# Eighteen query buffers in tiles of two groups, every store of two groups, and one gate for the accumulators

## The chip, the cores and the metric

The kernel runs on one core of a Trainium2 chip. A core has five engines with a queue of instructions each: TensorE (PE: matrix products into the accumulator memory PSUM), VectorE (DVE), ScalarE (ACT), GpSimd (POOL) and SyncE (SP, which here only issues transfers), and 16 DMA engines that move data between HBM and the on-chip memory SBUF. The engines run beside each other and are kept in step by semaphores alone. The metric is the device time of one execution in microseconds (us), lower is better. Three runs of the kernel before gave 128.72, 128.75 and 128.87 us, a median of 128.75.

## The reference

Every query of 8 x 12 heads attends to the same 16 keys and values of its head: those at positions 0, 64, 128, ... of 1024.

```python
def reference(Q, K, V, stride):                  # Q, K, V: (8, 12, 1024, 64) float32, stride 64
    attend_positions = np.arange(0, seq, stride)
    for i in range(seq):
        q = Q[:, :, i:i + 1, :]
        k = K[:, :, attend_positions, :]
        v = V[:, :, attend_positions, :]
        scores = np.einsum('bhqd,bhkd->bhqk', q, k) / np.sqrt(dim)
        weights = np.exp(scores - np.max(scores, axis=-1, keepdims=True))
        weights = weights / (np.sum(weights, axis=-1, keepdims=True) + 1e-10)
        result[:, :, i, :] = np.einsum('bhqk,bhkd->bhqd', weights, v)[:, :, 0, :]
```

Q is 25.2 MB and is read once, the result is as large and is written once. Of K and V only every 64th row is needed, 0.4 MB each.

## The kernel before, in words

**Tiling.** The 96 heads are taken as 24 groups of four heads (`NG` = 24). One group of Q is 1 MB, 2048 numbers on each of the 128 partitions. It is loaded into one of `BUFS` = 16 buffers `qn`, and when the group is done its output lies in the same buffer, from where it is stored. So group 16 can be loaded only when group 0 has been stored, since it takes the same buffer. The 16 buffers are four tiles `quad` of `RUN` = 4 buffers each, so that neighbouring groups lie side by side on a partition and one transfer (`send`) can store two or four of them.

**Stages of a group.** POOL casts the buffer to bf16 (`cast`, L306; the first three are shared with ACT, L300 and L302). DVE transposes it (L317). PE makes the scores in 16 products (`score_products`, L325). DVE takes the maximum and subtracts it (L339, L342). ACT takes the exponential (`raise_`, L347). DVE sums and inverts (L352, L355). POOL forms the weights (L359). PE transposes them in four products (`turn_products`, L366). ACT spreads them into a block form (`spread`, L378, two halves). PE multiplies with the values in eight products, four into either half of the accumulator tile `o` (`output_products`, L386). ACT copies the two halves of `o` to the buffer (`evict`, L406).

**The order.** The work is recorded in a fixed order, `ORDER`, one round per group, with a stage's number saying how many groups it lags. ACT's round is: spread of group i-3, eviction of both halves of group i-4, exponential of group i-1. PE runs a loop of two rounds per turn instead of a recorded list: scores of i, turning of i-2, output of i-3. The other engines' finished work reaches that loop through semaphores called gates: `turned` (DVE's transpose is there), `weighted` (POOL's weights are there), and `free0` and `free1` (ACT has emptied the first or the second half of `o`). The loop has 28 rounds for 24 groups; in the rounds past either end it multiplies data that nobody uses, and the tiles `k_t` and `v_all` are padded for them.

**Transfers.** All are issued by SP, in recorded order, through `_copy`, which builds the transfer instruction itself. First come the keys, group 0 of Q, the values, and groups 1 to 15. Then come the stores. `STORES` sets their sizes in groups, 4, 2, 2, 4, 4, 4, 2, 2; each is queued when its last group has been evicted. Behind the third store SP queues the loads of groups 16 to 23, each of which waits until the store of its buffer has landed. SP's queue is in order, so that nothing behind a waiting load is issued before it. The last store is sent from behind the recorded program, after all engines are done with it.

Of the kernel before, what the change touches and what calls it, by code (L numbers as in the profile page):

```python
# [10 lines left out]
FP32 = mybir.dt.float32  # L11
BF16 = mybir.dt.bfloat16
# [6 lines left out]
def _ap_with(ap: bass.AP, new_ap, extra_offset: int = 0) -> bass.AP:  # L19
    return dataclasses.replace(  # L20
        ap, ap=[list(p) for p in new_ap], offset=ap.offset + extra_offset
    )


def _copy(nc, out: bass.AP, in_: bass.AP):

    sides = [
        mybir.BassSymbolicTensorAccessPattern(
            ap=side.ap, dtype=side.dtype, bass_ap=side,
            is_dma=True, for_custom_bir_dma=True,  # L30
        )
        for side in (in_, out)
    ]
    return nc.sync.add_instruction(  # L34
        mybir.InstDMACopy(
            name=nc.get_next_instruction_name(), engine=mybir.EngineType.SP,
            ins=sides[:1], outs=sides[1:], queue="qSPDynamicHW",
            mode="Copy",
        )
    )  # L40


class Program:
# [125 lines left out]
def kernel(  # L169
# [29 lines left out]
    quads = [sb.tile([P, RUN, 32 * D], FP32, name=f"quad{i}") for i in range(BUFS // RUN)]  # L199
    qn = [quads[i // RUN][:, i % RUN] for i in range(BUFS)]  # L200
# [110 lines left out]
    def transpose(g):  # L311
        k_in = {0: "0", 1: "1"}.get(g)
        words = qt[g % 2].bitcast(I32)
        if g >= NG:
            op("DVE", lambda: nc.vector.memset(edge[:, g - NG : g - NG + 1], 0.0), gate="turned", times=1 if g == NG else 3)
# [42 lines left out]
    def weights(g):  # L358
        op("POOL", lambda: nc.gpsimd.tensor_tensor(  # L359
            out=wt[g % 2], in0=ex[g % 2],  # L360
            in1=rec[g % 2].unsqueeze(2).to_broadcast([P, 32, NK]), op=ALU.mult,
        ), reads=[f"ex{g % 2}", f"rec{g % 2}"] + [k for k in apart if k[0] == "v"], writes=[f"wt{g % 2}"], gate="weighted", times=1 if g < NG - 1 else 3)

    def turn_products(g):
        for c in range(4):
# [30 lines left out]
    def outputs(g, n):  # L396
        op("PE", None, reads=[f"wb{g % 2}0", f"wb{g % 2}1"] + [
               f"v{g % 2}{a}{b}{int(g >= 4)}" if 0 <= g < NG else "none" for a in range(2) for b in range(2)
           ], writes=[f"o{n}"], gates=[(f"free{n}", g + 1)] if g >= 0 else [], looped=True)

    def evict(g, n):
        to = qn[g % BUFS].rearrange("p (b c x d) -> p c b (x d)", b=2, c=4, d=D)
        half = slice(2 * n, 2 * n + 2)
        plain = g >= NG - 1 - 2 * n
        ready = [f"wb{(g + 1) % 2}0", f"wb{(g + 1) % 2}1"] * (n == 0)
        op("ACT", lambda: nc.scalar.copy(  # L406
            to[:, half], o_ps[:, half].rearrange("p c (b x) -> p c b x", b=2)
        ), reads=[f"o{n}"] + ready, writes=[f"qn{g % BUFS}{n}"],
           gate=None if plain else f"free{n}", last=g == NG - 1 and n == 1)

        if plain:
            free([f"qn{g % BUFS}{n}"], n)

    def free(reads, n):
        op("ACT", lambda: nc.scalar.nop(), reads=reads, gate=f"free{n}")  # L415

    def send(g, n):
        return _copy(
            nc,
            _ap_with(out, [[16 * D, P], [2 * SD, 2 * n], [1, 16 * D]], g * HG * SD),  # L420
            _ap_with(qn[g % BUFS], [quads[0].ap[0], [1, 1], [1, 32 * n * D]]),
        )

    def store(g, n):
# [40 lines left out]
    assert sum(STORES) == NG  # L465
    STORED = {sum(STORES[: i + 1]) - 1: n for i, n in enumerate(STORES)}

    def queue(g):
        if g not in STORED or g == NG - 1:
            return  # L470
        store(g - STORED[g] + 1, STORED[g])
        if g == NG - BUFS - 1:
            for n in range(BUFS, NG):
                load(n)

    def at(i, stage, lag):
        g = i - lag
        if g in early.get(stage, ()):
            return
        if stage == "transpose" and 0 <= g < NG + 2:  # L480
            transpose(g)
        elif stage == "scores" and 0 <= g < NG + 4:
            scores(g)
        elif stage == "weights" and 0 <= g < NG:
            weights(g)
        elif stage == "turn" and 0 <= g < NG + 2:
            turn(g)
        elif stage in ("outA", "outB") and -1 <= g < NG + 1:
            outputs(g, int(stage == "outB"))
        elif stage == "spread" and 0 <= g < NG:  # L490
            spread(g)
        elif stage in ("evA", "evB") and g == -1:
            n = int(stage == "evB")
            free(["wb00", "wb01"], n)
# [17 lines left out]
    def pe_stream(sems, gates):  # L512
        pe = nc.tensor
        done = sems["PE"]
        pe.sem_inc(gates["weighted"], 2)
        for n in range(2):
            pe.sem_inc(gates[f"free{n}"], 3)
        with pe.Fori(0, turns) as turn_:
            for j in range(TURN):
                i = turn_ * TURN + j  # L520
                pe.wait_ge(gates["turned"], j + 1)
                score_products(j, i).then_inc(done, 1)
                pe.wait_ge(gates["weighted"], j + 1)
                turn_products(j).then_inc(done, 1)
                for n in range(2):
                    pe.wait_ge(gates[f"free{n}"], j + 1)
                    output_products(j + 1, i, n).then_inc(done, 1)
            for name in ("turned", "weighted", "free0", "free1"):
# [11 lines left out]
_INS = ['Q', 'K', 'V', 'stride']  # L540
# [31 lines left out]
```

## Time and profile before

| | before |
|---|---|
| median of three runs | 128.75 us |
| the profiled execution: its time | 128.75 us |
| its span (first instruction to last) | 126.9 us |
| mean granted clock of TensorE | 0.86 |
| read, written | 25.95 MB, 25.17 MB |
| busy: PE / DVE / ACT / POOL | 66.9 / 88.0 / 97.6 / 75.9 us |

The span leaves out 1.85 us of the execution's time, which lie around it. The profile's page shows busy time by engine, the span in 40 slices of 3.17 us (a digit is the busy share in tenths), the DMA queues with the time that their packets took as a share of 16 engines' span, and the chain of work that ended last. A window table gives the same by stretches; its last two columns are the share of the 16 DMA engines that was busy (it can pass 1 for a short while, where one packet begins before the last one has ended) and the rate. In a timeline a row has its start, its length, engine, line, operation, tiles, and in brackets how long the engine had been idle and what released it. "SPq" is SyncE's queue: its rows are the issuing of transfers, not the transfers themselves.

### The profile page before, as it was taken

How to read it: one execution, taken by the hardware profiler on the slowest of the kernel's cores; microseconds unless marked ns; L12 is line 12 of the kernel's file. 1: busy time of each engine (PE TensorE's matmuls, PEld its weight loads, DVE VectorE, ACT ScalarE, POOL GpSimd, SP SyncE). 2: the span in 40 equal slices, each digit the busy share in tenths (PEclk: the TensorE clock that was granted, in tenths of full speed). 3: DMA queues.
4: the chain of work that ended last, by engine and by line, in shares of the span. 5: the costliest groups of instructions: out<-in, count | busy, mean ns of one | idle time of the engine just before them, and what ended most of it. 6: DMA issues, size and time to landing. Idle time of an engine off the chain costs nothing.

```text
span 126.9 us, 2253 instructions
## 1 busy us (share of the span) xinstructions
PE 66.9 (53%) x784; PEld 49.3 (39%) x784; DVE 88.0 (69%) x131; ACT 97.6 (77%) x133; POOL 75.9 (60%) x67
## 2 busy tenths in 40 slices
PE   0005796677836456586530394557856478771000
PEld 0004585455734334364320373335624356550000
DVE  3585979999899999999980779999999773000000
ACT  4147758999999999999993199999999999991000
POOL 5637698999999777797403996777793332000000
PEclk9999999965799999959996579998599955999755
DMA  0999999899998989989999999999999999999980
GB/s 23 418 320 465 392 454 465 372 475 392 444 475 361 465 361 485 454 351 423 418 470 434 413 454 392 465 434 403 454 385 457 423 423 444 392 398 434 429 382 21
DMA packets 5413, 51.16 MB, mean 403 GB/s; under 512 B 3616, under 2 KB 3616, under 8 KB 3616
## 3 DMA queue, kind: packets, MB, share of 16 engines
q1 hardware_dynamic: 5408, 51.12, 95.8%
q14 instruction: 5, 0.04, 0.1%
HBM read 25.95 MB, written 25.17 MB: 403 GB/s over the span
## 4 chain that ended last, share of the span: by engine, by line
DMA 30%; ACT 22%; POOL 21%; DVE 6%; issue 6%; PE 4%; SPq 1%; ACTq 0%; POOLq 0%
DMA out_dram<-quad 14%; ACT quad L406 13%; POOL qb L306 12%; DMA quad<-in_Q_dram 10%; ACT wb_all L378 7%; POOL wt_all L359 6%; DMA v_raw<-in_V_dram 6%; DVE qt L317 3%; ACT ex L347 3%; POOL v_all L288 2%; PE o L386 2%; DVE total L352 1%; SPq L34 1%; PE tp L366 1%; DVE top L339 1%
## 5 line engine op out<-in xcount | busy, mean ns | idle before, releaser
L406 ACT COPY quad<-o 128x1024 f32<-128x1024 f32 x48 | 46.3, 1015 | 2.2
L306 POOL CAST qb<-quad 128x2048 bf16<-128x2048 f32 x21 | 39.7, 1889 | 6.9 <-DMA quad<-in_Q_dram 6.8
L386 PE MATMUL o<-v_all,wb_all 128*128 x224 | 39.0, 317 | 2.4 <-ACTq L415 0.7
L359 POOL TENSOR_TENSOR wt_all<-ex,rec 128x512 bf16<-128x512 f32 x24 | 25.4, 1057 | 18.5 <-DVE rec L355 18.1
L378 ACT ACTIVATE wb_all<-tp,sel 128x512 bf16<-128x512 bf16 x48 | 30.4, 690 | 5.6 <-PE tp L366 5.4
L317 DVE STREAM_TRANSPOSE qt<-qb 128x1024 int32<-128x1024 int32 x24 | 29.7, 1237 | 5.2 <-POOL qb L306 5.0
L325 PE MATMUL sc<-k_t,qt 128*128 x448 | 23.3, 210 | 16.2 <-DVE qt L317 11.8
L325 PEld LDWEIGHTS sc<-k_t,qt 128*128 128x128 bf16 x448 | 20.4, 109 | 21.8 <-issue 19.6
L366 PE MATMUL tp<-identity,wt_all 128*128 128x128 bf16 x112 | 13.0, 249 | 29.8 <-POOL wt_all L359 29.8
L386 PEld LDWEIGHTS o<-v_all,wb_all 128*128 128x128 bf16 x224 | 22.9, 114 | 11.2 <-ACT quad L406 4.9
L352 DVE TENSOR_REDUCE total<-ex 128x32 f32<-128x512 f32 x24 | 16.3, 677 | 7.0 <-ACT ex L347 7.0
L366 PEld LDWEIGHTS tp<-identity,wt_all 128*128 128x128 bf16 x112 | 7.6, 109 | 32.6 <-POOL wt_all L359 32.6
L342 DVE TENSOR_TENSOR low<-sc,top 128x512 f32<-128x512 f32 x24 | 16.6, 691 | 0.8
L347 ACT ACTIVATE ex<-low 128x512 f32<-128x512 f32 x24 | 15.4, 641 | 2.1 <-DVE low L342 2.0
L339 DVE TENSOR_REDUCE top<-sc 128x32 f32<-128x512 f32 x24 | 15.2, 632 | 1.3 <-PE sc L325 1.3
L355 DVE RECIPROCAL rec<-total 128x32 f32<-128x32 f32 x24 | 8.5, 353 | 0.8
L288 POOL CAST v_all<-v_raw 32x128 bf16<-32x128 f32 (+1 forms) x12 | 5.2, 430 | 1.1 <-DMA v_raw<-in_V_dram 0.4
L302 POOL CAST qb<-quad 128x1024 bf16<-128x1024 f32 x3 | 3.1, 1037 | 4.3 <-DMA quad<-in_Q_dram 4.2
L300 ACT CAST qb<-quad 128x1024 bf16<-128x1024 f32 x3 | 3.1, 1045 | 2.4 <-DMA quad<-in_Q_dram 2.4
L264 ACT CAST k_half<-k_raw 128x768 bf16<-128x768 f32 x1 | 0.8, 831 | 3.2 <-DMA k_raw<-in_K_dram 3.2
L260 POOL MEMSET v_all<- 128x3584 f32 x1 | 3.1, 3085 | 0.0
L288 ACT CAST v_all<-v_raw 32x640 bf16<-32x640 f32 x4 | 2.9, 722 | 0.0
(15 smaller groups left out, 10.3 us busy)
## 6 DMA issues: line engine op xcount, KB each, us to landing
quad<-in_Q_dram SPq DMA_DIRECT2D x24, 1024.0 KB, 17.3
out_dram<-quad SPq DMA_DIRECT2D x4, 4096.0 KB, 18.3
out_dram<-quad SPq DMA_DIRECT2D x4, 2048.0 KB, 12.8
k_raw<-in_K_dram SPq DMA_DIRECT2D x1, 384.0 KB, 4.9
v_raw<-in_V_dram SPq DMA_DIRECT2D x1, 384.0 KB, 7.0
```

The lines of the kernel that those rows point to most:

```text
L306: op("POOL", lambda: nc.gpsimd.tensor_copy(out=b, in_=q), reads=[f"qn{g % BUFS}{h}" for h in range(2)] + apart, writes=[f"qb{g % 2}{h}" fo ...
L317: op("DVE", lambda: nc.vector.transpose(_ap_with(words, [words.ap[0], [1, 2], [D, 16], [2, 32]]), qb[g % 2].bitcast(I32),), reads=[f"qb{g ...
L325: r = nc.tensor.matmul(sc_ps[g % 2][:, 64 * i : 64 * i + 64], lhsT=_ap_with(qt[g % 2], [qt[g % 2].ap[0], [2, P]], extra_offset=2 * P * i + f),
L339: op("DVE", lambda: nc.vector.tensor_reduce(out=m, in_=s, op=ALU.max, axis=mybir.AxisListType.X,), reads=[f"sc{g % 2}"], writes=[f"top{g % ...
L342: op("DVE", lambda: nc.vector.tensor_tensor(out=low, in0=s, in1=m.unsqueeze(2).to_broadcast([P, 32, NK]), op=ALU.subtract,), reads=[f"sc{g ...
L347: op("ACT", lambda: nc.scalar.activation(out=ex[g % 2], in_=low, func=AF.Exp, bias=0.0, scale=scale,), reads=["low"], writes=[f"ex{g % 2}"])
L352: op("DVE", lambda: nc.vector.tensor_reduce(out=total[g % 2], in_=ex[g % 2], op=ALU.add, axis=mybir.AxisListType.X,), reads=[f"ex{g % 2}"] ...
L359: op("POOL", lambda: nc.gpsimd.tensor_tensor(out=wt[g % 2], in0=ex[g % 2], in1=rec[g % 2].unsqueeze(2).to_broadcast([P, 32, NK]), op=ALU.mult,
L366: r = nc.tensor.transpose(tp_ps[g % 2][:, 2 * c : 2 * c + 2].rearrange("p a b -> p (a b)"), wt[g % 2][:, 8 * c : 8 * c + 8].rearrange("p t ...
L378: op("ACT", lambda a=a: nc.scalar.activation(out=wb[g % 2][:, :, 64 * a : 64 * a + 64], in_=tp_ps[g % 2], func=AF.Copy, scale=sel[:, a : a ...
L386: r = nc.tensor.matmul(_ap_with(o_ps, [o_ps.ap[0], [128, 2], [256, 2], [1, D]], extra_offset=512 * c + D * u,), lhsT=wb[g % 2][:, 2 * c + ...
L406: op("ACT", lambda: nc.scalar.copy(to[:, half], o_ps[:, half].rearrange("p c (b x) -> p c b x", b=2)), reads=[f"o{n}"] + ready, writes=[f" ...
```

## The change

Four things change together.

- **Buffers and stores.** `BUFS` is 18 and `RUN` is 2: nine tiles `pair` of two buffers. All twelve stores have two groups. Eighteen groups of Q are loaded ahead of the first store; the loads of the remaining six come in pairs, with one more store queued between a pair and the store that it waits for. The store of groups 20 and 21 is queued one group later than the others.
- **Keys and values** are loaded by the language's ordinary call (`nc.sync.dma_start`) instead of `_copy`, with the same access patterns on both sides. In the built program the two instructions differ from the ones before in a single mark, "precooked".
- **PE's loop** has 26 rounds instead of 28; the output of the last group is made behind the loop. The gates that stood for three counts at the end are back to one.
- **One gate for the accumulators**: `free` is raised once per group, by the eviction of the second half, and PE waits for it once, ahead of all eight output products. Before, the first four needed only the first half.

In SP's queue before, the stretch from the first store to the fourth (quad0 holds groups 0 to 3, then 16 to 19; "at_ACT" is ScalarE's progress, "at_out0of4" the landing of the first store):

```order
L34 DMA out_0_dram<-quad0_62 128x8x1024 [waits at_ACT]
L34 DMA out_0_dram<-quad1_63 128x4x1024 [waits at_ACT] x2
L34 DMA quad0_62<-in_Q_dram 128x2048 [waits at_out0of4]
L34 DMA quad0_62<-in_Q_dram 128x2048 x3
L34 DMA quad1_63<-in_Q_dram 128x2048 [waits at_out2of2]
L34 DMA quad1_63<-in_Q_dram 128x2048
L34 DMA quad1_63<-in_Q_dram 128x2048 [waits at_out3of2]
L34 DMA quad1_63<-in_Q_dram 128x2048
L34 DMA out_0_dram<-quad2_64 128x8x1024 [waits at_ACT]
```

And in the changed kernel, the same stretch (pair0 holds groups 0 and 1, then 18 and 19):

```order
L34 DMA out_0_dram<-pair0_62 128x4x1024 [waits at_ACT]
L34 DMA out_0_dram<-pair1_63 128x4x1024 [waits at_ACT]
L34 DMA pair0_62<-in_Q_dram 128x2048 [waits at_out0of2]
L34 DMA pair0_62<-in_Q_dram 128x2048
L34 DMA out_0_dram<-pair2_64 128x4x1024 [waits at_ACT]
L34 DMA pair1_63<-in_Q_dram 128x2048 [waits at_out1of2]
L34 DMA pair1_63<-in_Q_dram 128x2048
L34 DMA out_0_dram<-pair3_65 128x4x1024 [waits at_ACT]
L34 DMA pair2_64<-in_Q_dram 128x2048 [waits at_out2of2]
L34 DMA pair2_64<-in_Q_dram 128x2048
L34 DMA out_0_dram<-pair4_66 128x4x1024 [waits at_ACT]
```

Before, eight loads stand in one block between stores; now three blocks of two loads alternate with stores of two groups.

On PE, the end of one round before (the eight output products, in two halves):

```order
L366 MATMUL tp0_91<-identity_74,wt_all_87 128x128 [waits gate_weighted]
L366 MATMUL tp0_91<-identity_74,wt_all_87 128x128 x3
L386 ISA [waits gate_free0]
L386 MATMUL o_93<-v_all_77,wb_all_88 128x2x2x64 x4
L386 MATMUL o_93<-v_all_77,wb_all_88 128x2x2x64 [waits gate_free1]
L386 MATMUL o_93<-v_all_77,wb_all_88 128x2x2x64 x3
```

And in the changed kernel:

```order
L365 MATMUL tp0_96<-identity_79,wt_all_92 128x128 [waits gate_weighted]
L365 MATMUL tp0_96<-identity_79,wt_all_92 128x128 x3
L385 ISA [waits gate_free]
L385 MATMUL o_98<-v_all_82,wb_all_93 128x2x2x64 x8
```

The wait for the second half of the eviction has moved ahead of the first four products. The core of the diff:

```diff
-    BUFS = 16
-    RUN = 4
+    BUFS = 18
+    RUN = 2
...
-    k_t = sb.tile([P, NG + 4, 2, 4 * NK], BF16, name="k_t")
-    v_all = sb.tile([P, NG + 4, 4, D], BF16, name="v_all")
+    k_t = sb.tile([P, NG + 2, 2, 4 * NK], BF16, name="k_t")
+    v_all = sb.tile([P, NG + 3, 4, D], BF16, name="v_all")
...
     def load_rows(name, tile_, src, lane):
-        op("SP", lambda: _copy(
-            nc, tile_, _ap_with(src, kv_src),
-        ), writes=[name], lane=lane)
+        op("SP", lambda: nc.sync.dma_start(tile_, _ap_with(src, kv_src)),
+           writes=[name], lane=lane)
...
-           ], writes=[f"o{n}"], gates=[(f"free{n}", g + 1)] if g >= 0 else [], looped=True)
+           ], writes=[f"o{n}"], gates=[("free", g + 1)] if g >= 0 and not n else [], looped=True)
...
-        plain = g >= NG - 1 - 2 * n
-        ready = [f"wb{(g + 1) % 2}0", f"wb{(g + 1) % 2}1"] * (n == 0)
         op("ACT", lambda: nc.scalar.copy(
             to[:, half], o_ps[:, half].rearrange("p c (b x) -> p c b x", b=2)
-        ), reads=[f"o{n}"] + ready, writes=[f"qn{g % BUFS}{n}"],
-           gate=None if plain else f"free{n}", last=g == NG - 1 and n == 1)
-
-        if plain:
-            free([f"qn{g % BUFS}{n}"], n)
+        ), reads=[f"o{n}"], writes=[f"qn{g % BUFS}{n}"], gate="free" if n and g < NG - 1 else None,
+           last=g == NG - 1 and n == 1)
...
-    turns = (NG + 4) // TURN
-
-    STORES = [4, 2, 2, 4, 4, 4, 2, 2]
+    turns = (NG + 2) // TURN
...
     def queue(g):
-        if g not in STORED or g == NG - 1:
-            return
-        store(g - STORED[g] + 1, STORED[g])
-        if g == NG - BUFS - 1:
-            for n in range(BUFS, NG):
-                load(n)
+        if g == NG - RUN:
+            store(g - RUN, RUN)
+        elif g % RUN == RUN - 1 and g < NG - RUN - 1:
+            store(g - RUN + 1, RUN)
+            late = BUFS + g - 2 * RUN + 1
+            if BUFS <= late < NG:
+                for n in range(late, late + RUN):
+                    load(n)
...
+                pe.wait_ge(gates["free"], j + 1)
                 for n in range(2):
-                    pe.wait_ge(gates[f"free{n}"], j + 1)
                     output_products(j + 1, i, n).then_inc(done, 1)
...
+        pe.wait_ge(gates["free"], 1)
+        for n in range(2):
+            output_products(NG - 1, NG + 2, n).then_inc(done, 1)
...
-    end = send(NG - STORES[-1], STORES[-1])
+    end = send(NG - RUN, RUN)
```

More of the change, by code (lines that the diff above doesn't have):

```diff
@@ L198 @@
     edge = sb.tile([P, 32], FP32, name="edge")
-    quads = [sb.tile([P, RUN, 32 * D], FP32, name=f"quad{i}") for i in range(BUFS // RUN)]
-    qn = [quads[i // RUN][:, i % RUN] for i in range(BUFS)]
+    pairs = [sb.tile([P, RUN, 32 * D], FP32, name=f"pair{i}") for i in range(BUFS // RUN)]
+    qn = [pairs[i // RUN][:, i % RUN] for i in range(BUFS)]
     k_raw = sb.tile([P, NC, D], FP32, name="k_raw")
@@ L314, in transpose @@
         if g >= NG:
-            op("DVE", lambda: nc.vector.memset(edge[:, g - NG : g - NG + 1], 0.0), gate="turned", times=1 if g == NG else 3)
+            op("DVE", lambda: nc.vector.memset(edge[:, g - NG : g - NG + 1], 0.0), gate="turned")
             return
@@ L361, in weights @@
             in1=rec[g % 2].unsqueeze(2).to_broadcast([P, 32, NK]), op=ALU.mult,
-        ), reads=[f"ex{g % 2}", f"rec{g % 2}"] + [k for k in apart if k[0] == "v"], writes=[f"wt{g % 2}"], gate="weighted", times=1 if g < NG - 1 else 3)
+        ), reads=[f"ex{g % 2}", f"rec{g % 2}"] + [k for k in apart if k[0] == "v"], writes=[f"wt{g % 2}"], gate="weighted")
     def turn_products(g):
@@ L403, in evict @@
         half = slice(2 * n, 2 * n + 2)
-        plain = g >= NG - 1 - 2 * n
-        ready = [f"wb{(g + 1) % 2}0", f"wb{(g + 1) % 2}1"] * (n == 0)
         op("ACT", lambda: nc.scalar.copy(
             to[:, half], o_ps[:, half].rearrange("p c (b x) -> p c b x", b=2)
-        ), reads=[f"o{n}"] + ready, writes=[f"qn{g % BUFS}{n}"],
-           gate=None if plain else f"free{n}", last=g == NG - 1 and n == 1)
-        if plain:
-            free([f"qn{g % BUFS}{n}"], n)
-    def free(reads, n):
-        op("ACT", lambda: nc.scalar.nop(), reads=reads, gate=f"free{n}")
+        ), reads=[f"o{n}"], writes=[f"qn{g % BUFS}{n}"], gate="free" if n and g < NG - 1 else None,
+           last=g == NG - 1 and n == 1)
     def send(g, n):
@@ L420, in send @@
             _ap_with(out, [[16 * D, P], [2 * SD, 2 * n], [1, 16 * D]], g * HG * SD),
-            _ap_with(qn[g % BUFS], [quads[0].ap[0], [1, 1], [1, 32 * n * D]]),
+            _ap_with(qn[g % BUFS], [pairs[0].ap[0], [1, 1], [1, 32 * n * D]]),
         )
@@ L460 @@
     VALUES.update((i + 2, [large[4 + i]]) for i in range(4))
-    turns = (NG + 4) // TURN
-    STORES = [4, 2, 2, 4, 4, 4, 2, 2]
-    assert sum(STORES) == NG
-    STORED = {sum(STORES[: i + 1]) - 1: n for i, n in enumerate(STORES)}
+    turns = (NG + 2) // TURN
     def queue(g):
-        if g not in STORED or g == NG - 1:
-            return
-        store(g - STORED[g] + 1, STORED[g])
-        if g == NG - BUFS - 1:
-            for n in range(BUFS, NG):
-                load(n)
+        if g == NG - RUN:
[6 more added lines that the diff above has]
+                    load(n)
     def at(i, stage, lag):
@@ L481, in at @@
             transpose(g)
-        elif stage == "scores" and 0 <= g < NG + 4:
+        elif stage == "scores" and 0 <= g < NG + 2:
             scores(g)
@@ L485, in at @@
             weights(g)
-        elif stage == "turn" and 0 <= g < NG + 2:
+        elif stage == "turn" and 0 <= g < NG:
             turn(g)
-        elif stage in ("outA", "outB") and -1 <= g < NG + 1:
+        elif stage in ("outA", "outB") and -1 <= g < NG:
             outputs(g, int(stage == "outB"))
@@ L491, in at @@
             spread(g)
-        elif stage in ("evA", "evB") and g == -1:
-            n = int(stage == "evB")
-            free(["wb00", "wb01"], n)
+        elif stage == "evB" and g == -1:
+            op("ACT", lambda: nc.scalar.nop(), reads=["wb00", "wb01"], gate="free")
         elif stage in ("evA", "evB") and 0 <= g < NG:
@@ L515, in pe_stream @@
         pe.sem_inc(gates["weighted"], 2)
-        for n in range(2):
-            pe.sem_inc(gates[f"free{n}"], 3)
+        pe.sem_inc(gates["free"], 3)
         with pe.Fori(0, turns) as turn_:
@@ L524, in pe_stream @@
                 turn_products(j).then_inc(done, 1)
+                pe.wait_ge(gates["free"], j + 1)
                 for n in range(2):
-                    pe.wait_ge(gates[f"free{n}"], j + 1)
                     output_products(j + 1, i, n).then_inc(done, 1)
-            for name in ("turned", "weighted", "free0", "free1"):
+            for name in ("turned", "weighted", "free"):
                 pe.sem_inc(gates[name], -TURN)
+        pe.wait_ge(gates["free"], 1)
+        for n in range(2):
+            output_products(NG - 1, NG + 2, n).then_inc(done, 1)
     pending, sems = prog.emit(pe_stream)
```

## The prediction

> **What bounds the kernel now.** I read the page first: the slices, the DMA queues and the read and written bytes.
>
> ```profile
> ACT  4147758999999999999993199999999999991000
> ...
> DMA  0999999899998989989999999999999999999980
> ...
> q1 hardware_dynamic: 5408, 51.12, 95.8%
> ...
> HBM read 25.95 MB, written 25.17 MB: 403 GB/s over the span
> ```
>
> The DMA engines are busy from the second slice to the last but one: 95.8% of 126.9 us is 121.6 us of work on all 16, and the change moves the same bytes. ACT, the busiest engine, has a hole in slices 22 and 23 and has ended by slice 37. So the second view is the table by windows, cut where loads and stores alternate. The columns read here are the last two, DMA share and GB/s.
>
> ```profile
> 20.00:40.00 20.00, 12.86 (x162) 10.16 (x159) 18.77 (x30) 19.28 (x28) 19.37 (x16) 0.83 0.98 423
> ...
> 56.00:64.00 8.00, 5.44 (x65) 3.73 (x62) 7.28 (x11) 7.83 (x13) 4.91 (x4) 0.92 1.01 426
> 64.00:67.00 3.00, 0.70 (x18) 0.55 (x16) 2.28 (x4) 2.91 (x4) 0.00 (x0) 1.00 1.08 448
> ...
> 68.00:84.00 16.00, 8.75 (x107) 6.46 (x108) 11.80 (x17) 11.37 (x16) 13.37 (x9) 0.80 0.99 426
> 84.00:89.00 5.00, 2.81 (x40) 1.98 (x36) 4.66 (x9) 4.83 (x8) 3.44 (x3) 0.90 0.99 419
> ...
> 95.00:111.00 16.00, 11.19 (x132) 8.19 (x132) 8.74 (x17) 15.44 (x22) 4.27 (x5) 0.79 1.00 424
> ...
> 116.00:121.00 5.00, 0.00 (x0) 0.00 (x0) 0.00 (x0) 0.00 (x0) 0.00 (x0) 0.77 0.99 423
> ...
> 123.00:127.00 4.00, 0.00 (x0) 0.00 (x0) 0.00 (x0) 0.00 (x0) 0.00 (x0) 0.50 0.14 57
> ```
>
> Loads (20 to 40, 68 to 84), stores of two groups (56 to 64, 116 to 121) and of four (95 to 111) all run at 423 to 426 GB/s with every DMA engine busy. Nothing is fed late until 123 us, where a few late engines finish alone. DMA is the bound from beginning to end; what the compute engines gain counts only if DMA waits for it.
>
> **Does DMA wait for compute?** The place to look is the loads of groups 16 to 23. POOL's and ACT's timelines around the hole:
>
> ```profile
> 55.08 1.89 POOL L306 CAST qb<-quad 128x2048 bf16<-128x2048 f32 x1
> ...
> 58.77 1.89 POOL L306 CAST qb<-quad 128x2048 bf16<-128x2048 f32 x1
> ...
> 68.76 1.89 POOL L306 CAST qb<-quad 128x2048 bf16<-128x2048 f32 x1 [6.24 <-DMA quad<-in_Q_dram]
> ...
> 65.22 1.93 ACT L406 COPY quad<-o 128x1024 f32<-128x1024 f32 x2
> ...
> 73.72 1.93 ACT L406 COPY quad<-o 128x1024 f32<-128x1024 f32 x2
> ```
>
> A round lasts 3.69 us (55.08 to 58.77). The cast of group 16 waits 6.24 us for its load, and the next eviction comes 8.50 us after the last, 4.8 us late. The change removes this hole if its loads land in time. The last loads issued ahead in before, and the landings of stores (the wait of the next load shows them), come from these rows (the second line is the time from issue to landing of the two loads in the first):
>
> ```profile
> L34 SPq DMA_DIRECT2D quad<-in_Q_dram x2: 593/594/594, 13.9 to 14.5; - x2
> ...
> DMA to landing us min/median/max: 29.8/30.7/31.6
> ...
> 38.13 17.85 DMA out_dram<-quad
> ...
> 55.99 0.53 SPq L34 DMA_DIRECT2D quad<-in_Q_dram  x1
> ...
> 61.03 0.47 SPq L34 DMA_DIRECT2D quad<-in_Q_dram  x1
> ...
> 66.29 1.11 SPq L34 DMA_DIRECT2D quad<-in_Q_dram  x2
> ```
>
> Group 15 lands at 14.5 + 31.6 = 46.1 us, group 14 at 43.7: 2.44 us a load. The stores land at 55.98, 61.0 and 66.3: 9.9 us for four groups, 5.0 and 5.3 for two. I take 5.1 for two groups. The changed order then runs: 18 loads until 51.0, store 0-1 until 56.1, store 2-3 until 61.2, loads 18 and 19 until 66.1, store 4-5 until 71.2, loads 20 and 21 until 76.1, store 6-7 until 81.2, loads 22 and 23 until 86.1, then eight stores. Without a hole casts would follow 58.77 at 3.69 us: group 16 at 62.5, 18 at 69.8, 20 at 77.2, 22 at 84.6. Their loads land at 48.6, 63.7, 73.6 and 83.7. All are in time, the tightest by 0.9 us, so the hole goes.
>
> **What that is worth.** The end of the program, from the issues of the last two stores, each with its time to landing:
>
> ```profile
> 108.95 0.54 SPq L34 DMA_DIRECT2D out_dram<-quad  x1
> ...
> DMA to landing us min/median/max: 12.3/12.3/12.3
> ...
> 115.78 0.54 SPq L34 DMA_DIRECT2D out_dram<-quad  x1
> ...
> DMA to landing us min/median/max: 10.4/10.4/10.4
> ```
>
> The last store is issued at 115.8 but lands at 126.2, and the one before it lands at 121.25. DMA thus comes to the last store 5.5 us after it was issued. Issued 4.8 us earlier, at 111.0, it waits 10.3 us instead of 5.5. The hole's gain on the end is 0: it is covered by the stores queued ahead, and it would count only if those were gone. The later queueing of store 20-21 (one round, 3.69 us) is covered by the same queue.
>
> **The other parts.**
>
> Stores of two groups for the four of four groups. 16.8 MB go over at another size, 39.6 us at 424 GB/s. By share of busy engines the rows give 426 / 1.01 = 422 against 424 / 1.00, 0.5% of 39.6 us: +0.2. The ends: the two-group pairs at 5.0 and 5.3 (mean 5.15) against 9.9 / 2 = 4.95 give eight times 0.2, +1.6. The last pair, 121.25 to 126.2, took 4.95, with no compute engine beside it; against 5.1 that gives eight times -0.15, -1.2. I take +0.2, since both its windows lie beside compute, as most stores do.
>
> Changes of direction. Loads and stores now alternate in seven places instead of three. The window with the change from stores to loads (64 to 67) moved 448 GB/s, no loss; the one with the change to stores (84 to 89) 419 against 426, 0.08 us over 5 us. Four more: 0 to +0.3, taken as +0.1, nearer the row without loss.
>
> Compute ends earlier. Stores that land while ACT works take 5.0 to 5.3 us a pair and the last pair took 4.95; about one pair more falls behind ACT's end: -0.2. The ends are 0 and -0.4.
>
> The ordinary call. Its effect is not in this trace; the rows of the first issues are these (the last line is the keys' time from issue to landing):
>
> ```profile
> 0.95 0.73 SPq L34 DMA_DIRECT2D k_raw<-in_K_dram  x1
> 1.74 0.83 SPq L34 DMA_DIRECT2D quad<-in_Q_dram  x1
> 2.61 0.62 SPq L34 DMA_DIRECT2D v_raw<-in_V_dram  x1
> ...
> L34 SPq DMA_DIRECT2D quad<-in_Q_dram x24: 471/596/2307, 1.7 to 66.8; - x24
> ...
> DMA to landing us min/median/max: 4.9/4.9/4.9
> ```
>
> Nothing runs on the DMA engines before the keys, so what their issue saves or loses shifts the whole chain. It can save at most its 0.73 us; at the other end, as long as the longest load issue (2.31), it loses 1.6. I take -0.2: the issues that follow a wait (55.99, 61.03) last 0.47 to 0.53. The values' issue and 0.62 us of it are covered by the keys' and group 0's transfers.
>
> One gate. PE's round and ACT's beside it:
>
> ```profile
> 46.74 1.93 ACT L406 COPY quad<-o 128x1024 f32<-128x1024 f32 x2
> ...
> 47.80 0.40 PE L366 MATMUL tp<-identity,wt_all 128*128 128x128 bf16 x4 [0.84 <-POOL wt_all L359]
> 48.03 1.30 PE L386 MATMUL o<-v_all,wb_all 128*128 x8
> 49.18 0.73 PE L325 MATMUL sc<-k_t,qt 128*128 x16
> ...
> 50.43 1.93 ACT L406 COPY quad<-o 128x1024 f32<-128x1024 f32 x2
> ...
> 51.49 0.40 PE L366 MATMUL tp<-identity,wt_all 128*128 128x128 bf16 x4 [1.58 <-POOL wt_all L359]
> ```
>
> The eight products now start when the eviction ends, at 48.7 instead of 48.03. Behind the waiting products PE has the scores, then the turning. Products until 50.0, scores until 50.7, and the weights come at 51.5: still 0.7 us idle. ACT next wants the first half at 50.43, and it is there by about 49.4. Cost 0, covered by PE's idle 1.58 us a round; without that cover it is half of 1.30, 0.65 us a round.
>
> The loop of 26 rounds and smaller pads: PE's dead rounds (after 113) and the fills of the first 5 us lie beside DMA work. 0. The last output products behind the loop come near 110, with 10.3 us of queued stores ahead: 0.
>
> **The sum** is made against the profiled execution, 128.75 us (span 126.9 and 1.85 around it), which is also the median: -0.2 + 0.2 + 0.1 - 0.2 gives 128.65, given as 128.7. This kernel's runs can tell a change of about 0.2%, 0.26 us, from none.
>
> A rule to weigh here, first the rows: landings of two-group stores queued one behind the other are 4.95 to 5.3 us apart. The Trainium skill (DMA: Bandwidth & Descriptors, Anatomy of one DMA) gives, for transfers issued by GpSimd, a fixed 2.0 us for each plus its bytes at 436 GB/s, most of it spent on confirming the last write. Four more transfers would by that add 8 us, and the sum would be near 136.7; landings would be 6.8 us apart. The trace doesn't agree for SP's queue while further work is queued. By the page the fixed part would come back where a queue runs dry, which is the third rival.
>
> **The rivals.**
>
> *Smaller stores run worse among loads.* Stores of two groups take 5.15 us beside compute, not 4.95, or each change of direction costs its 0.08: eight times 0.1 to 0.2 and four times 0.08, about +1.0: 129.7. For it speaks the landing at 66.3 (5.3 us); against it 426 GB/s in the same stretch.
>
> *The single gate becomes the round's bound* (the other side). If the 0.65 us adds to all 23 rounds it makes 15 us; 10.3 are free, so +4.7: 133.4. It decides from 10.3 / 23 = 0.45 us a round. Against it stand PE's 0.7 us that remain.
>
> *DMA runs dry at a waiting load.* When store 0-1 lands, one store, 5.1 us, is queued; a load issued then needs its way in. The keys took 4.9 us from issue to landing, of which 0.39 MB at 424 GB/s are 0.9, so at most 4.0. It decides beyond 5.1, and 1 us lost at each of the three waits gives 131.7.
>
> *Stores of two groups are faster.* All at the last pair's 4.95: -1.2 in place of +0.2, 127.3. Against it: that pair had no compute beside it.
>
> *The ordinary call.* Gaining its 0.73 whole gives 128.1; losing 1.6 gives 130.4.
>
> **How the numbers follow.** My forecast, the sum with its own range of 128.3 to 129.0, has 0.55: of it 0.14 lie below 128.49, 0.36 within 0.26 us of before, 0.05 above. Worse stores have 0.14, the gate 0.05, the dry queue 0.05, faster stores 0.12, the call 0.05 for its gain and 0.04 for its loss. Faster: 0.14 + 0.12 + 0.05 = 0.31. Same: 0.36. Slower: 0.05 + 0.14 + 0.05 + 0.05 + 0.04 = 0.33. The range 127.2 to 130.0 takes in the worse stores, the call's gain and the faster stores; it leaves out the gate, the dry queue and the call's loss, 0.14, and the outer ends of the others.
>
> **What would show it.** In the profile after, DMA should stay at 9 tenths to the last slices at 420 to 426 GB/s, with 36 rather than 32 of SP's Q loads and stores; POOL's cast should wait for no load after the first microseconds; ACT should end near 110 and the last store be issued near 111 and land some 15 us later. PE's output products should start at the end of the eviction with rounds still 3.69 us apart. I am wrong if a window between 50 and 90 shows a DMA share well below 1, if rounds lengthen beyond 4.1 us, if stores of two groups land more than 5.2 us apart all along, or if the first load's packets come at another time by more than 0.3 us.

## The result, and the profile after

The changed kernel takes 128.11 us (six runs, 127.91 to 128.31) against 128.75 before (128.66 to 128.87): a ratio of 0.9949, 95% interval 0.9938 to 0.9961, or 0.64 us less. It lies in the stated range of 127.2 to 130.0, but below the 128.3 to 129.0 that I gave for the forecast itself. The profiled execution took 128.15 us with a span of 126.4.

The page of the changed kernel, the rows that answer to those shown of before:

```profile
ACT  4257739999999999999999999999999975000000
...
DMA  1999989899897999999999999989999999999991
...
q1 hardware_dynamic: 5984, 51.12, 96.5%
...
k_raw<-in_K_dram SPq DMA_DIRECT2D x1, 384.0 KB, 4.3
v_raw<-in_V_dram SPq DMA_DIRECT2D x1, 384.0 KB, 6.8
```

ACT's hole is gone and ACT ends in slice 34 instead of 37. DMA still works from end to end, so most of that is worth nothing. 96.5% of 126.4 us is 122.0 us of packets against 121.6 before: the smaller stores cost 0.4 us of DMA time. The keys land 4.3 us after their issue instead of 4.9.

The window table of the changed kernel: loads (20 to 40), stores of two groups (86 to 122), and the end.

```profile
20.00:40.00 20.00, 10.01 (x159) 8.24 (x159) 19.08 (x30) 19.25 (x28) 19.43 (x17) 1.00 1.00 429
...
86.00:106.00 20.00, 11.46 (x132) 8.54 (x132) 9.56 (x18) 19.01 (x26) 6.26 (x6) 0.91 1.01 427
106.00:122.00 16.00, 0.00 (x0) 0.00 (x0) 0.00 (x0) 0.00 (x0) 0.00 (x0) 0.54 1.01 427
```

After 106 us nothing but DMA is at work, at the same 427 GB/s as beside the compute. SyncE's timeline at both ends, the last line being the last store's time to landing:

```profile
0.96 0.43 SPq L236 DMA_DIRECT2D k_raw<-in_K_dram  x1
1.45 0.74 SPq L34 DMA_DIRECT2D pair<-in_Q_dram  x1
2.24 0.71 SPq L236 DMA_DIRECT2D v_raw<-in_V_dram  x1
...
L34 SPq DMA_DIRECT2D out_dram<-pair x1: 538/538/538, 106.5 to 106.5; - x1
...
DMA to landing us min/median/max: 19.1/19.1/19.1
```

The keys' issue takes 0.43 us instead of 0.73, and group 0's issue behind it starts 0.29 us earlier. The first packet of the keys starts 2.08 us after the span's start instead of 2.46. The last store is issued at 106.5, 9.3 us earlier than before, and lands at 125.6, 0.6 earlier. The compute gained 9 us and the end of the transfers 0.6. Where a store of two groups follows another, they land 5.1 to 5.3 us apart on the last DMA engine until 101 us, beside the compute, and 4.9 to 5.0 from then on.

GpSimd's, ScalarE's and TensorE's timelines late in the program, and one row of the waits:

```profile
78.19 1.89 POOL L305 CAST qb<-pair 128x2048 bf16<-128x2048 f32 x1
...
83.32 1.89 POOL L305 CAST qb<-pair 128x2048 bf16<-128x2048 f32 x1 [1.58 <-DMA pair<-in_Q_dram]
...
87.88 1.93 ACT L403 COPY pair<-o 128x1024 f32<-128x1024 f32 x2
...
90.20 1.28 ACT L377 ACTIVATE wb_all<-tp,sel 128x512 bf16<-128x512 bf16 x2
91.34 1.96 ACT L403 COPY pair<-o 128x1024 f32<-128x1024 f32 x2
...
93.44 1.04 PE L385 MATMUL o<-v_all,wb_all 128*128 x8 [0.42 <-ACT pair L403]
...
PE o L385 <- ACT pair L403: 8.2, 18, 1.9
```

One wait for a load is left, 1.58 us at group 22. It is there because rounds are shorter than I planned with: 3.46 us from one eviction to the next (87.88 to 91.34) instead of 3.69. TensorE does wait at the single gate, 8.2 us in 18 waits; ScalarE's evictions wait for TensorE in turn for 0.7 us in all, by the page's group of L403. ScalarE's eviction at 91.34 begins before its spreading (90.20 to 91.48) has ended. Before, the spreading below had ended at 50.35 when the eviction began at 50.43:

```profile
49.08 1.27 ACT L378 ACTIVATE wb_all<-tp,sel 128x512 bf16<-128x512 bf16 x2
```

### The profile page after: what moved, and what is told of

Read it like the earlier page. It is cut to its first block, busy times and chain, and to the rows that moved or that the text cites. A ratio compares the mean times of both kernels' runs of the same rounds, so it can differ in the third digit from the quotient of the medians.

```text
span 126.4 us, 2107 instructions
## 1 busy us (share of the span) xinstructions
PE 58.6 (46%) x736; PEld 44.9 (36%) x736; DVE 88.0 (70%) x131; ACT 95.2 (75%) x133; POOL 75.8 (60%) x67
## 3 DMA queue, kind: packets, MB, share of 16 engines
q1 hardware_dynamic: 5984, 51.12, 96.5%
## 4 chain that ended last, share of the span: by engine, by line
DMA 47%; ACT 18%; POOL 8%; DVE 7%; SPq 2%; issue 1%; PE 1%; POOLq 0%
DMA out_dram<-pair 31%; ACT pair L403 10%; DMA pair<-in_Q_dram 10%; ACT wb_all L377 6%; DMA v_raw<-in_V_dram 5%; POOL qb L305 3%; DVE qt L316 3%; POOL wt_all L358 2%; POOL v_all L287 2%; ACT ex L346 2%; SPq L34 2%; DVE total L351 1%; DVE top L338 1%; DVE rec L354 1%; POOL qb L301 1%
## 5 line engine op out<-in xcount | busy, mean ns | idle before, releaser
L403 ACT COPY pair<-o 128x1024 f32<-128x1024 f32 x48 | 49.7, 1168 | 0.7 <-PE o L385 0.7
L305 POOL CAST qb<-pair 128x2048 bf16<-128x2048 f32 x21 | 39.7, 1891 | 2.3 <-DMA pair<-in_Q_dram 2.1
L385 PE MATMUL o<-v_all,wb_all 128*128 (+1 forms) x216 | 31.9, 297 | 8.2 <-ACT pair L403 8.2
L377 ACT ACTIVATE wb_all<-tp,sel 128x512 bf16<-128x512 bf16 x48 | 33.6, 823 | 1.3 <-PE tp L365 0.8
L324 PE MATMUL sc<-k_t,qt 128*128 x416 | 19.9, 204 | 11.3 <-DVE qt L316 11.1
L324 PEld LDWEIGHTS sc<-k_t,qt 128*128 128x128 bf16 x416 | 17.7, 105 | 15.2 <-issue 14.3
L346 ACT ACTIVATE ex<-low 128x512 f32<-128x512 f32 x24 | 19.0, 792 | 2.2 <-DVE low L341 2.2
L301 POOL CAST qb<-pair 128x1024 bf16<-128x1024 f32 x3 | 3.1, 1039 | 3.8 <-DMA pair<-in_Q_dram 3.8
L299 ACT CAST qb<-pair 128x1024 bf16<-128x1024 f32 x3 | 3.1, 1044 | 2.4 <-DMA pair<-in_Q_dram 2.4
L259 POOL MEMSET v_all<- 128x3456 f32 x1 | 3.0, 2979 | 0.0
(15 smaller groups left out, 10.2 us busy)
```

Of the source, the lines that this page charges most:

```text
L305: op("POOL", lambda: nc.gpsimd.tensor_copy(out=b, in_=q), reads=[f"qn{g % BUFS}{h}" for h in range(2)] + apart, writes=[f"qb{g % 2}{h}" fo ...
L324: r = nc.tensor.matmul(sc_ps[g % 2][:, 64 * i : 64 * i + 64], lhsT=_ap_with(qt[g % 2], [qt[g % 2].ap[0], [2, P]], extra_offset=2 * P * i + f),
L346: op("ACT", lambda: nc.scalar.activation(out=ex[g % 2], in_=low, func=AF.Exp, bias=0.0, scale=scale,), reads=["low"], writes=[f"ex{g % 2}"])
L377: op("ACT", lambda a=a: nc.scalar.activation(out=wb[g % 2][:, :, 64 * a : 64 * a + 64], in_=tp_ps[g % 2], func=AF.Copy, scale=sel[:, a : a ...
L385: r = nc.tensor.matmul(_ap_with(o_ps, [o_ps.ap[0], [128, 2], [256, 2], [1, D]], extra_offset=512 * c + D * u,), lhsT=wb[g % 2][:, 2 * c + ...
L403: op("ACT", lambda: nc.scalar.copy(to[:, half], o_ps[:, half].rearrange("p c (b x) -> p c b x", b=2)), reads=[f"o{n}"], writes=[f"qn{g % B ...
```

## The experiments

Ratios are to the kernel before, run on the same chip in the same rounds; 0.001 is 0.13 us.

**The call for keys and values, put into the kernel before.**

```diff
-        op("SP", lambda: _copy(nc, tile_, _ap_with(src, kv_src)), ...)
+        op("SP", lambda: nc.sync.dma_start(tile_, _ap_with(src, kv_src)), ...)
```

> The kernel before with only the call for keys and values changed. If the gain of 0.64 us is made at the head (the keys' issue took 0.43 us instead of 0.73, and group 1 landed 0.31 us earlier on the median DMA engine and 0.58 on the last), this kernel takes 128.1 to 128.4. If the gain comes from the stores of two groups and their effect on the slowest DMA engine, it stays at 128.6 to 128.8.

128.16 us against 128.59, ratio 0.9961 (0.9948 to 0.9975). The keys' row shows the same short issue:

```profile
0.96 0.43 SPq L236 DMA_DIRECT2D k_raw<-in_K_dram  x1
```

The call alone makes 0.5 us (0.3 to 0.7), as the theory of the head expected. In its trace the first packet of the keys starts at 2.07 us, against 2.46 before: the whole chain of transfers begins 0.39 us sooner. (Its profiled execution, 128.88, was its slowest one; the last DMA engine ends 2.75 us behind the median one there, against 2.0 before.) The values' issue, by the same call, isn't shorter: 0.57 us here and 0.71 in the changed kernel, against 0.62 before.

**The same call taken out of the changed kernel** (the diff above, reversed).

> The changed kernel with keys and values loaded as before. If the call makes the gain, 128.6 to 128.9, and the keys' issue is back at 0.7 us. If the stores make it, 128.1 to 128.3.

128.33 us, ratio 0.9982 (0.9966 to 0.9998), between the two expectations. The keys' issue is back, and the first packet starts at 2.47 us:

```profile
0.95 0.73 SPq L34 DMA_DIRECT2D k_raw<-in_K_dram  x1
```

0.9982 against 0.9949 is 0.42 us for the call once more. But some 0.2 us of gain stays without it, so that the call isn't the whole.

**Buffers and stores alone.**

```diff
-    BUFS = 16
-    RUN = 4
+    BUFS = 18
+    RUN = 2
...
-    STORES = [4, 2, 2, 4, 4, 4, 2, 2]
+    STORES = [2] * 12
...
-        if g == NG - BUFS - 1:
-            for n in range(BUFS, NG):
-                load(n)
+        late = BUFS + g - 2 * RUN + 1
+        if BUFS <= late < NG:
+            for n in range(late, late + RUN):
+                load(n)
```

> The kernel before with eighteen buffers in pairs, all stores of two groups and the loads of groups 18 to 23 in pairs between them; its call for keys and values, its two gates and its 28 rounds stay. If the stores cost what the prediction's sum says (+0.2 for their size, +0.1 for turns, -0.2 for the earlier end of compute), 128.6 to 129.0. If they make the gain, 128.1 to 128.3. Either way POOL's wait of 6 us for group 16's load is gone.

128.68 us, ratio 1.0004 (0.9988 to 1.0019): nothing. Its group of POOL's casts:

```profile
L306 POOL CAST qb<-pair 128x2048 bf16<-128x2048 f32 x21 | 39.7, 1891 | 0.6 <-DMA pair<-in_Q_dram 0.6
```

The waits for loads fall from 6.8 us to 0.6, and the time doesn't move. That the hole is worth nothing is shown.

**Single gate and loop of 26 rounds.**

```diff
-           ], writes=[f"o{n}"], gates=[(f"free{n}", g + 1)] if g >= 0 else [], looped=True)
+           ], writes=[f"o{n}"], gates=[("free", g + 1)] if g >= 0 and not n else [], looped=True)
...
-    turns = (NG + 4) // TURN
+    turns = (NG + 2) // TURN
```

> The kernel before with only the single gate and the loop of 26 rounds; sixteen buffers, stores of four and two groups and the call for keys and values stay. The DMA engines are the bound, so every theory that puts the gain into the transfers expects 128.6 to 128.9 here; ACT's rounds stay 3.7 us apart. If the gate costs its 0.65 us a round, compute ends 10 us or more later and the time is over 132.

128.24 us, ratio 0.9977 (0.9955 to 0.9999). This was below what all theories of the transfers expected, and the rounds were 3.47 us. So I took the two apart. (In this kernel and in the two below with 26 rounds and the old sizes of stores, the store of groups 20 and 21 also stands one group later in SyncE's queue, as in the change. It lands 4.9 us behind the one ahead of it with and without that, so it still comes out of a waiting queue.)

**The gate alone, 28 rounds.**

```diff
-        ready = [f"wb{(g + 1) % 2}0", f"wb{(g + 1) % 2}1"] * (n == 0)
...
-        ), reads=[f"o{n}"] + ready, writes=[f"qn{g % BUFS}{n}"],
+        ), reads=[f"o{n}"], writes=[f"qn{g % BUFS}{n}"],
...
+                pe.wait_ge(gates["free"], j + 1)
                 for n in range(2):
-                    pe.wait_ge(gates[f"free{n}"], j + 1)
```

> The kernel before with only the single gate; its 28 rounds, its stores and its call for keys and values stay. Single gate plus short loop took 128.24 against 128.59 (ratio 0.9977), with ACT's rounds 3.47 us apart instead of 3.70. If the shorter rounds are the gate's work (its eviction no longer waits for ACT's own spreading), the rounds here are 3.47 too; if a shorter compute also leaves the slowest DMA engine less behind, 128.2 to 128.4. If compute off the bound is worth nothing, 128.5 to 128.7 with rounds of 3.47.

128.54 us, ratio 0.9996 (0.9985 to 1.0007): no gain. ScalarE's timeline in this kernel:

```profile
45.92 2.00 ACT L405 COPY quad<-o 128x1024 f32<-128x1024 f32 x2
...
49.39 2.03 ACT L405 COPY quad<-o 128x1024 f32<-128x1024 f32 x2
```

The rounds are 3.47 us, so the shorter round is the gate's work. Its two half gates came with `ready`: the first half's eviction waited until ScalarE's own spreading had ended. With one gate, raised by the second half, that wait is dropped and the two overlap. Dropping the wait without joining the gates wasn't run. Either way it is worth nothing here.

**The loop alone, both gates kept.**

```diff
-    turns = (NG + 4) // TURN
+    turns = (NG + 2) // TURN
...
+        for n in range(2):
+            pe.wait_ge(gates[f"free{n}"], 1)
+            output_products(NG - 1, NG + 2, n).then_inc(done, 1)
```

(with the pads of `k_t` and `v_all` cut as in the change)

> The kernel before with only the loop of 26 rounds and smaller pads; both gates stay, and with them the eviction's wait for the spreading. If the gate makes the shorter rounds, they are 3.70 us here and the time is 128.5 to 128.7. If the short loop and the smaller pads make the gain, 128.2 to 128.4.

128.27 us, ratio 0.9979 (0.9967 to 0.9990): 0.27 us, with rounds of 3.70 us. Two rows of its timeline and the windows at the end of the kernel before and of this one:

```profile
46.60 1.93 ACT L404 COPY pair<-o 128x1024 f32<-128x1024 f32 x2
...
50.30 1.93 ACT L404 COPY pair<-o 128x1024 f32<-128x1024 f32 x2
```

Before:

```profile
110.00:116.00 6.00, 3.99 (x56) 2.77 (x56) 0.00 (x0) 4.26 (x5) 0.00 (x0) 1.00 0.98 418
```

With 26 rounds:

```profile
110.00:116.00 6.00, 1.65 (x8) 0.74 (x8) 0.00 (x0) 3.85 (x4) 0.00 (x0) 0.67 0.94 399
```

TensorE's dead products are gone (56 matmuls in the window, now 8). Nobody waits for them, and yet the end moves. The rate of this one window isn't what to read (from 106 to 116 us it is 415 GB/s before and 419 here). The landings are: two stores of four groups, those of groups 12 to 15 and 16 to 19, each with its time to landing. Before:

```profile
L34 SPq DMA_DIRECT2D out_dram<-quad x1: 591/591/591, 87.3 to 87.3; - x1
...
DMA to landing us min/median/max: 18.8/18.8/18.8
...
L34 SPq DMA_DIRECT2D out_dram<-quad x1: 538/538/538, 102.1 to 102.1; - x1
...
DMA to landing us min/median/max: 14.3/14.3/14.3
```

With 26 rounds:

```profile
L34 SPq DMA_DIRECT2D out_dram<-pair x1: 591/591/591, 87.2 to 87.2; - x1
...
DMA to landing us min/median/max: 18.8/18.8/18.8
...
L34 SPq DMA_DIRECT2D out_dram<-pair x1: 539/539/539, 102.0 to 102.0; - x1
...
DMA to landing us min/median/max: 14.0/14.0/14.0
```

The second store, beside which the dead products lay, lands 10.3 us after the first before and 10.0 now. The trace has 16 landings for each transfer, one for each DMA engine: by these the last engine took 10.29 us and now takes 9.99, while the median engine takes 9.81 and 9.82. The other traces agree: 10.29 and 10.16 in the two other kernels above with 28 rounds and these stores (the call alone, the gate alone), 9.88 and 9.98 in the two with 26 (gate and loop, and the next one). The smaller pads, which also went, don't show: with gate and loop the loads ahead land at 46.2 us, as before (46.1).

**Call, gate and loop, without the new stores.**

```diff
-        op("SP", lambda: _copy(nc, tile_, _ap_with(src, kv_src)), ...)
+        op("SP", lambda: nc.sync.dma_start(tile_, _ap_with(src, kv_src)), ...)
...
-    turns = (NG + 4) // TURN
+    turns = (NG + 2) // TURN
...
+                pe.wait_ge(gates["free"], j + 1)
```

> The kernel before with the ordinary call for keys and values, the single gate and the loop of 26 rounds, but with its sixteen buffers and stores of four and two groups. If the parts add up (call -0.43, gate and loop -0.35, stores of two about 0), this takes about 127.8 beside 128.6 of before, no slower than the whole change. If the gain of gate and loop was only noise, 128.1 to 128.3.

127.73 us, ratio 0.9935 (0.9918 to 0.9952). The parts add up. It is no slower than the whole change (0.9949, 0.9938 to 0.9961); the intervals overlap, so that it is faster isn't shown.

**Why dead products cost time: the transfers alone.**

```diff
     def op(engine, *rest, **more):
+        if engine == "SP":
+            return full(engine, *rest, **more)
```

> The transfers of the kernel before, all of them in its order and sizes, with the compute left out (the groups are stored as they were loaded). The floor of the transfers: if compute beside the stores is what slows single DMA engines, the last engine ends less than 0.8 us behind the median one (before: 2.0) and the time is 127.0 to 127.8. If the lag belongs to the transfers themselves, it is 1.5 to 2.5 us and the time 128.4 to 128.8.

127.12 us, ratio 0.9884 (0.9863 to 0.9905): the compute beside them costs the transfers about 1.5 us, although DMA is busy throughout in both. Its profiled execution took 128.35, the longest of five (the others 127.08 to 127.25), with one DMA engine late from group 0's load on, so only the distances between landings are read from it. That engine is 1.7 us behind the median one before the first store and 1.8 at the end: an engine can be late with no compute at all, but here it doesn't fall further behind while it stores. Before, the lag grows from 0.5 us to 2.0. The next four kernels put one engine's work back at a time.

**TensorE's work beside the transfers.**

```diff
+        with pe.Fori(0, 17) as turn_:
+            for j in range(TURN):
+                score_products(j, j)
+                turn_products(j)
+                for n in range(2):
+                    r = output_products(j, j, n)
```

> The transfers alone (127.12 us, where every store of four groups landed 9.80 to 9.85 us after the one ahead of it on the last DMA engine) with 34 rounds of TensorE's products beside them, on filled tiles and waiting for nothing; nothing else is computed. If TensorE's work beside the stores is what holds the last DMA engine back (10.2 to 10.3 us with the whole compute), its landings are 10.2 us apart while TensorE runs and the time is about 128.0 to 128.5. If not, 9.8 to 9.9 and 127.0 to 127.3.

128.31 us, ratio 0.9972 (0.9954 to 0.9989): 1.1 us over the transfers alone.

**ScalarE's, VectorE's and GpSimd's work, each alone.**

```diff
-        if engine == "SP":
+        if engine == "SP" or engine == "ACT" and "writes" in more:
```

(against the transfers alone; for the other two the line is `if engine in ('SP', 'DVE'):` and `if engine in ('SP', 'POOL'):`, and the tiles that nobody computes are filled first)

> The transfers alone with ScalarE's whole work beside them, in its order and on filled tiles; the stores wait for its copies, the other engines compute nothing. If ScalarE's work holds the last DMA engine back, stores of four groups land 10.2 us apart and the time is about 128.0 to 128.5; if not, 9.8 to 9.9 and 127.0 to 127.3.

> The transfers alone with VectorE's whole work beside them on filled tiles, until about 95 us. If VectorE's work holds the last DMA engine back, the stores up to 95 us land 10.2 us apart for four groups and the time is 127.6 to 128.2; if not, 9.8 to 9.9 and 127.0 to 127.3.

> The transfers alone with GpSimd's whole work beside them, its casts reading the loaded buffers, until about 95 us. If GpSimd's work holds the last DMA engine back, the stores up to 95 us land 10.2 us apart for four groups and the time is 127.6 to 128.2; if not, 9.8 to 9.9 and 127.0 to 127.3.

127.63 us (0.9930, 0.9912 to 0.9947), 127.43 (0.9916, 0.9896 to 0.9936) and 127.21 (0.9902, 0.9886 to 0.9919). SyncE's loads behind the waits for the first and the second store show when the last DMA engine had landed them. In order: the transfers alone, with TensorE, with ScalarE, with VectorE, with GpSimd.

```profile
57.22 1.20 SPq L34 DMA_DIRECT2D quad<-in_Q_dram  x2
62.13 1.12 SPq L34 DMA_DIRECT2D quad<-in_Q_dram  x2
```

```profile
56.46 1.81 SPq L34 DMA_DIRECT2D quad<-in_Q_dram  x3
61.75 1.12 SPq L34 DMA_DIRECT2D quad<-in_Q_dram  x2
```

```profile
55.60 2.71 SPq L34 DMA_DIRECT2D quad<-in_Q_dram  x4
60.51 1.17 SPq L34 DMA_DIRECT2D quad<-in_Q_dram  x2
```

```profile
56.16 1.90 SPq L34 DMA_DIRECT2D quad<-in_Q_dram  x3
61.08 1.12 SPq L34 DMA_DIRECT2D quad<-in_Q_dram  x2
```

```profile
55.73 2.74 SPq L34 DMA_DIRECT2D quad<-in_Q_dram  x4
60.64 1.18 SPq L34 DMA_DIRECT2D quad<-in_Q_dram  x2
```

The store of two groups takes 4.91, 5.29, 4.91, 4.92 and 4.91 us. Only TensorE's work stretches this one. The windows with TensorE show that it was busy all of that time, and that it had stopped later:

```profile
46.00:66.00 20.00, 20.00 (x363) 18.86 (x362) 0.00 (x0) 0.00 (x0) 0.00 (x0) 1.00 1.00 422
...
85.00:105.00 20.00, 0.00 (x0) 0.00 (x0) 0.00 (x0) 0.89 (x2) 0.00 (x0) 0.50 0.99 424
```

After the loads come three stores of four groups, issued at 68.67, 69.43 and 77.07 (the first two share a row, with the shorter and the longer of their times to landing):

```profile
L34 SPq DMA_DIRECT2D out_dram<-quad x2: 591/968/1346, 68.7 to 69.4; - x2
...
DMA to landing us min/median/max: 27.9/32.5/37.0
...
L34 SPq DMA_DIRECT2D out_dram<-quad x1: 10307/10307/10307, 77.1 to 77.1; - x1
...
DMA to landing us min/median/max: 39.1/39.1/39.1
```

They land at 96.6, 106.4 and 116.2: 9.8 us apart, 4.9 for two groups, once TensorE rests. Beside the whole compute in the kernel before, the same stores landed at 95.9, 106.1 and 116.4, 10.2 and 10.3 apart. By engine, in the kernel with TensorE alone, the last one took 10.60 and 5.29 us for the first two stores and the median one 9.87 and 4.94; its lag grows from 0.2 to 1.5 us over the first three stores and stays at 1.8 once TensorE has stopped. The mean rate of all 16 DMA engines hardly shows it, because it is the last engine that is held back, and a store has landed only when its last engine has.

The expectations of the ScalarE and VectorE kernels missed by 0.1 to 0.3 us in their times, and the landings by engine place most of that. With VectorE the last engine is 0.7 us behind the median one before the first store and still 0.7 at the end, so that VectorE's work beside the stores added nothing. With ScalarE it falls from 0.6 to 1.05 us behind in a single store, that of groups 8 to 11: 10.31 us on the last engine, 9.84 on the median one. ScalarE was busy beside the other stores too, and they took 9.87, 4.91 and 9.82. One store in one trace doesn't tell whether ScalarE's work did it, so that a small part of ScalarE's isn't excluded. With GpSimd the lag is 0.3 us after the loads ahead and 0.5 at the end, and no store added to it.

What stays open: why TensorE's work should hold back a DMA engine that stores. The runs don't tell.

## Why the prediction was right, and where it was wrong

The time is within the range, but the sum was -0.1 and the result is -0.64, so that two of its terms have to be named. The range of the forecast itself, 128.3 to 129.0, doesn't hold it; the wide one does, because it reached down for other reasons (the call's whole gain, faster stores), and that is luck.

*DMA is the bound throughout*: right. The windows after keep 427 GB/s, and 9 us of earlier compute are 0.6 us at the end.

*The hole goes and is worth 0*: right, by the run with stores and buffers alone. *The loads arrive in time*: nearly; 1.58 us of waiting remained at group 22, whose load landed at 83.2 us (planned: 83.7), because the shorter rounds asked for it sooner. For the same reason the last store was issued at 106.5 us and not near 111.

*Stores, changes of direction, earlier end (+0.2, +0.1, -0.2, together +0.1)*: measured +0.05 (-0.15 to +0.24), within what the sum can claim. The single terms weren't separated; the 5.1 us taken for a store of two groups beside compute was about right (5.1 to 5.3).

*One gate, 0*: right in time (ratio 0.9996). "Rounds still 3.69 us apart" was wrong. I had looked at what the gate makes TensorE wait for, and not at what the two gates had made ScalarE wait for.

*The ordinary call, -0.2*: the mechanism was right and the size was off. It measured -0.42 to -0.5. I took the row of Q's loads behind a wait (0.47 to 0.53 us) as nearest; the keys' issue came to 0.43, 0.30 less than before, and the first packet started 0.38 us sooner. That is more than the 0.3 us that the prediction had named as a sign of being wrong. That the keys land 4.3 us after their issue instead of 4.9 can't be put down to the call: kernels with the old call have 4.4 to 5.0.

*The loop of 26 rounds, 0*: this step failed. That PE's dead rounds "lie beside DMA work" was true (they begin at 110.2 us, though, not after 113) and was no reason for a price of nothing: taking them out gave 0.27 us (0.13 to 0.42). The runs show in its place that TensorE's work beside stores costs the last DMA engine time. In the kernel with TensorE alone, 20 us of its work beside stores cost 1.1 us (the loads ahead of them kept their 2.44 us each). An estimate from that is 0.05 us a microsecond, and 0.1 us for the 2.3 us of work that left the window from 110 to 116. The traces put 0.30 us into the one store beside which that work lay (10.29 to 9.99 us on the last engine). So the place is shown; why it is more than the estimate stays open.

By measured parts: call -0.42 to -0.5, loop -0.27, gate and stores 0 make -0.7 to -0.8, against -0.64 of the whole, within the intervals. Of the rivals, only the call's gain came, and in part: that its 128.1 is also the result is luck, since 0.27 us of it is the loop's. DMA didn't run dry (a share of 0.97 or more in each 10 us from 50 to 90), the stores of two groups were neither worse nor faster, and TensorE's wait at the single gate cost nothing. The late engines stood in the table I had quoted (0.14 of the DMA engines still busy from 123 to 127 us), and I passed over them.

The rule of the Trainium skill that I weighed (DMA: Bandwidth & Descriptors, Anatomy of one DMA: a fixed cost for each transfer, given there for those that GpSimd issues) would have made the four further stores dear. In these runs, where SyncE issues them and its queue held the next transfer, they are free (ratio 1.0004 with the stores alone).

## What to carry to other kernels

Where transfers are the bound from end to end, what is left to gain lies where nothing runs beside them: the first issue, and the DMA engine that ends last. An operation that nobody waits for can still cost time through what it does to a shared resource, so "it lies beside other work" prices it at nothing only if the other work is not slowed; take it out once and look. And where a gate is moved, read the waits on both sides of it.

## What the runs showed of the hardware that I had not expected

TensorE's products held back the last of the DMA engines while it stored: 5.29 us for a store of two groups against 4.91 without, and 1.1 us on the program, on data that no transfer touches. Beside ScalarE's, VectorE's and GpSimd's work the same store took 4.91 to 4.92; one later store of four groups beside ScalarE took 10.31 against 9.8.

The same keys' load, with the same access patterns, is issued in 0.43 us by the ordinary call and in 0.73 by the hand-built instruction, and its first packet starts at 2.07 to 2.08 us instead of 2.46 to 2.47. For the values' load, third in the queue, no gain shows (0.57 and 0.71 us against 0.62).

Two ScalarE instructions overlap when the second doesn't wait for the first: the eviction began 0.14 us before the spreading had ended, and the round fell from 3.70 to 3.47 us, though the rows' own durations grew (a half eviction's mean from 1015 to 1168 ns).
